# Loads, stores and pacing of the pair operands in a two-layer encoder trunk, with the SwiGLU's row scale and the query loads placed elsewhere

## The chip, the cores and the metric

The kernel runs on one core of a Trainium2 chip. Its time is the device time of one execution in microseconds (us). TensorE is called PE here, VectorE DVE, ScalarE ACT, GpSimd POOL and SyncE SP, as in the profile.

## The reference

Two request groups, one of 1024 tokens ("p", the prompt, token blocks 1 and 2 of 512 tokens) and one of 512 ("s", block 0), go through the same two layers with the same weights, in float32. Each layer is a mixer with a residual, then a SwiGLU with a residual:

```python
for i in range(DEPTH):                      # DEPTH = 2, D_MODEL = 1024, D_FF = 2816
    if i % 2 == 0:
        x = x + fourier_mixer(x, norm_mix[i], fourier_w[j])
    else:                                   # 8 query heads, 2 key heads of 128
        x = x + attention_mixer(x, norm_mix[i], attn_w_qkv[j], attn_q_norm[j],
                                attn_k_norm[j], attn_w_o[j], cos, sin)
    x = x + swiglu_ffn(x, norm_ffn[i], ffn_w_gate[i], ffn_w_up[i], ffn_w_down[i])

def swiglu_ffn(x, g, w_gate, w_up, w_down):
    h = rms_norm(x, g)
    return (jax.nn.silu(h @ w_gate) * (h @ w_up)) @ w_down
```

`rms_norm` divides each token's row by its root mean square and multiplies by a gain. The two groups don't depend on each other.

## The kernel before

**Numbers.** Activations lie with features on partitions and tokens on the free axis: a block of 512 tokens is 8 chunks of 128 x 512. Each operand of a product is split into a rounded high part and the rest (`split`, L238: ACT casts, L242, and DVE or POOL subtracts, L243). A product is three matmuls, high by high, high by low, low by high (`mm3`, L249 to L251). Weights come from DRAM by `weights_by` (L278): loads issued on SP (L283), a cast on ACT (L287), a subtraction on POOL (L288).

**Two ways of the SwiGLU.** Block 0 goes through `ffn` (L759): 22 blocks (`fc`) of 128 hidden features, each with a gate product, an up product and the element-wise part: gate by the row scale `first["r"]` on DVE (L851), up by the row scale on DVE (L852), silu on ACT (L853), silu by up on DVE (L854), and a split into `mid`. The down products of two blocks at a time wait in a list, `pend`, and are slipped between the gate and up matmuls of the next block; their results are added up on DVE (L780). Blocks with odd `fc` close a pair. Blocks 1 and 2 go through `ffn_pair` (L924), which multiplies the two blocks, and two halves of every weight, as 2 x 2 matrices of blocks with seven products in place of eight. The seven operands of the activation side (`OPERANDS`: B11, B21, T2, T1, B22, T3, N4) are sums and differences of normed chunks of the two token blocks.

**Making the pair operands.** `moving` (L871) makes them in four rounds `j`. A round loads four residual chunks (two token blocks, two halves of the features) from DRAM into one buffer `x4` (L883, on SP), multiplies them by gain and row scale on DVE (L889), and forms the operands in three thirds: first B11, B21 and B22, then T1 and T3, then T2 and N4 (subtractions on DVE, L912 to L919). `put` splits each operand; B21, T1, T3 and N4 have their subtraction on POOL (`helped`), the others on DVE. Each split operand is stored to DRAM at once (L905, on SP). B11 and B21 also stay in the `ring` in SBUF. Every third ends with `yield 5.0`. `x4` and the buffer of T2 and N4 have the same tag, `wX`, with four buffers (`BUFS`, L151).

**Weaving.** Stages are Python generators. `weave` (L1397) runs two of them, a main and an aux one. Each `yield` states a cost; the one whose stated costs are the smaller share of its whole cost goes next. So the yields set where in the program text a stage's instructions stand among the other's. In layer 0 main is `ffn` of block 0 (whole cost 352) and aux the prompt's Fourier mixer, its projection and `moving` (250). In layer 1 main is block 0's attention and `ffn` (223 + 0.85 x 352 = 522.2) and aux the prompt's attention, output projection and `moving` (630). Behind `moving`, `paired` (L1515) emits the pair's first weights; when the weave is over, the rest of `ffn_pair` is emitted.

**Order and buffers.** The order of the text is a priority, not the order of the queues: when the program is built, each engine is given, among the instructions that are ready, the one that stands first in the text. On the chip each engine works through its queue in that order, and waits where an input has not come. Buffers of one tag are handed out in the order of the text.

**Down weights of the pair.** For each pair of blocks `f0`, `load_rows_down` (L997) loads two rows of the down weight at step T1, `prepare_down` (L1031) starts their sums and splits at step B22 (first DVE product at L1017, first POOL one at L1019), and the generator behind it is continued at T3 and later.

**Attention.** `attend` (L1307) takes, for each of the 8 heads, a query (loads on SP, L1333, split by ACT and POOL), then for each 128 queries the scores, the softmax, transposed probabilities and the values. The query of a head is loaded and split at the head's start.

Of the kernel before, what the change touches and what calls it, by code (L numbers as in the profile page):

```python
# [20 lines left out]
TB = 512  # L21
# [104 lines left out]
def trunk_kernel(ctx: ExitStack, tc: tile.TileContext, t: dict):  # L126
# [632 lines left out]
    def ffn(layer, b, h, out=None):  # L759
        h = h()  # L760
        here = b in resident
        acc = resident.pop(b) if here else staying[b]
        kept[b] = acc
        yield 0.0

        def halves(ms, wds, f0, dc):

            box = []

            def half(i):  # L770
                w = wds[dc // 4].rearrange("p h (f c) n -> p h f c n", f=2)
                mm3(box[0], w[:, 0, i, dc % 4], w[:, 1, i, dc % 4], ms[i][:, 0], ms[i][:, 1], i == 0, i == 1)

            def begin():
                box.append(bank())
                half(0)

            def end():
                half(1)
                dve.tensor_tensor(acc[dc], box[0], acc[dc], op=ALU.add)  # L780
                if f0 + 2 == NF:
                    new_residual(b, dc, acc[dc], None if out is None else out[:, dc, :])

            return begin, end

        def one(n=1):
            for _ in range(n):
                if pend:
                    pend.pop(0)()

        ready = {v: first[i] for i, v in enumerate((("gate", 0), ("up", 0), ("gate", 1)))} if here else {}

        def want(v, fc):
            if fc < NF and (v, fc) not in ready:
                ready[v, fc] = weights(down_src(layer, fc, "AB".index(v)) if v in "AB" else t[v][layer, fc])

        def open_items(ms, f0):

            wds = [ready.pop(("A", f0))]
            pairs = [halves(ms, wds, f0, dc) for dc in range(NC)]  # L800
            turns = [pairs[0][0], pairs[1][0], pairs[0][1], pairs[1][1]]
            for v in pairs[2:]:
                turns.extend(v)
            pend.extend(turns)
            return wds

        wds = None
        want("gate", 0)
        want("up", 0)
        for fc in range(NF):  # L810
            f0, odd_ = fc - fc % 2, fc % 2
            wg, wu = ready.pop(("gate", fc)), ready.pop(("up", fc))
            if not odd_ and wds is not None:
                want("B", f0 - 2)
                wds.append(ready.pop(("B", f0 - 2)))
            ga, up = bankg(), bankg()
            for dc in range(NC):
                if odd_ and dc == 4:
                    want("A", f0)
                part(wg, h, ga, dc)  # L820
                if here and fc == 0:
                    part(wu, h, up, dc)
                if not odd_ and dc >= 5:
                    one()
                if dc % 2:
                    yield 1.36 if odd_ or dc < 5 else 2.0 if dc == 5 else 2.7
            if odd_:
                want("gate", fc + 1)
                wds = open_items(ms, f0)
            for dc in range(NC):  # L830
                if not odd_ and dc == 3:
                    want("gate", fc + 1)
                if fc == NF - 1 and dc == 4:
                    want("B", f0)
                if dc == (2 if odd_ else 4):
                    want("up", fc + 1)
                if fc == 0 and not here and dc == 1:
                    settled(b)
                if not (here and fc == 0):
                    part(wu, h, up, dc)  # L840
                if not odd_:
                    one(2 if dc in (2, 4, 6) else 1)
                elif dc >= 6:
                    one()
                if dc % 2:
                    yield (3.4 if dc > 1 else 2.7) if not odd_ else 2.7 if dc == 7 else 1.36
            s = tmp()
            if fc == 0 and not here:
                first["r"] = tl("ss", [TB], F32, "ssF")
                act.copy(first["r"], in_rows(rstd[b]))  # L850
            dve.tensor_tensor(ga, ga, first["r"], op=ALU.mult)  # L851
            dve.tensor_tensor(up, up, first["r"], op=ALU.mult)  # L852
            act.activation(s, ga, AF.Silu)  # L853
            dve.tensor_tensor(up, up, s, op=ALU.mult)  # L854
            m = tl("mid", [2, TB], F32R, "mid")
            split(m[:, 0], m[:, 1], up)
            if odd_:
                ms.append(m)
            else:
                ms = [m]  # L860
        want("B", NF - 2)
        wds.append(ready.pop(("B", NF - 2)))
# [8 lines left out]
    def moving(blocks, gain, out, ring, helped):  # L871

        staging = open_pool("mv")
        yield 2.0
        r = [in_rows(rstd[b]) for b in blocks]
        yield 1.0
        for j in range(4):
            x4 = tl("x", [2, 2, TB], F32, "wX")
            v = {}
            for k in range(2):  # L880
                for d in range(2):
                    x = x4[:, d, k]
                    sp.dma_start(x, xres[blocks[k]][:, 4 * d + j, :])  # L883
                    v[d, k] = x
            a2 = bank2()
            for (d, k), x in list(v.items()):
                if d == k:
                    v[d, k] = a2[:, d]
                dve.scalar_tensor_tensor(v[d, k], x, gain[:, 4 * d + j : 4 * d + j + 1], r[k], op0=ALU.mult, op1=ALU.mult)  # L889
            room = []  # L890

            def put(name, src):
                if name in OPERANDS[:2]:
                    x = ring[:, 4 * OPERANDS.index(name) + j]
                elif name == "T1":
                    x = tl("l", [2, TB], F32R, "rawX")
                elif name in ("B22", "T3"):
                    x = tl("l", [2, TB], F32R, "mv", staging)
                else:
                    if not room:  # L900
                        two = tl("l", [2, 2, TB], F32R, "wX")
                        room.extend([two[:, 0], two[:, 1]])
                    x = room.pop(0)
                split(x[:, 0], x[:, 1], src, eng=pool if name in helped else None)
                sp.dma_start(out[name][:, j], x.bitcast(F32))  # L905

            put("B11", v[0, 0])
            put("B21", v[1, 0])
            put("B22", v[1, 1])
            yield 5.0  # L910
            t1 = x4[:, 0, 0]
            dve.tensor_tensor(t1, v[0, 1], v[0, 0], op=ALU.subtract)  # L912
            put("T1", t1)
            dve.tensor_tensor(v[0, 1], v[1, 1], v[0, 1], op=ALU.subtract)
            put("T3", v[0, 1])
            yield 5.0
            dve.tensor_tensor(v[1, 1], v[1, 1], t1, op=ALU.subtract)
            put("T2", v[1, 1])
            dve.tensor_tensor(v[1, 0], v[1, 0], v[1, 1], op=ALU.subtract)  # L919
            put("N4", v[1, 0])  # L920
            yield 5.0
        close_pool("mv")

    def ffn_pair(layer, blocks, ring, places, outs):  # L924
# [106 lines left out]
        def prepare_down(f0):  # L1031

            preps.append(operands_down(f0))
            next(preps[-1])
# [140 lines left out]
        for f0 in range(0, NF, 2):  # L1175
# [20 lines left out]
                plus(U[i], ps, U[i])  # L1196
            for i, ps in (yield from step("T1", lambda: load_rows_down(f0), 0)):
                plus(V[i], ps, U[i])
            for i, ps in (yield from step("B22", lambda: prepare_down(f0), 0)):
                plus(ps, ps, V[i])  # L1200
                if i == 0:
                    s = gated(1, W, ps)
                else:
                    finish(1, ps, s)
            for i, ps in (yield from step("T3", lambda: next(preps[-1]), 0)):
                plus(U[i], ps, U[i])
                plus(ps, ps, V[i])
                if i == 0:
                    s = gated(2, V[0], ps)
                else:  # L1210
                    finish(2, ps, s)
            for i, ps in (yield from step("N4", None if f0 else lambda: load_acc(blocks[0], 0), 0)):
                plus(ps, ps, U[i])
                if i == 0:
                    s = gated(3, U[0], ps)
# [91 lines left out]
    def attend(blocks, straight, slot):  # L1307
# [6 lines left out]
        for g in range(NKV):  # L1314
# [12 lines left out]
                sp.dma_start(vr[:, n * 4 : n * 4 + 4], dv[b][g][:, :, :])  # L1327
            split(vt[:, 0], vt[:, 1], vr, eng=pool)
            yield 1.0
            for h in range(g * GROUP, (g + 1) * GROUP):  # L1330
                qr = raw_tile(T)
                for n, b in enumerate(blocks):
                    sp.dma_start(qr[:, n * TB : (n + 1) * TB], dqk[b][h][:, :])  # L1333
                qt = w_tile(2, T)
                split(qt[:, 0], qt[:, 1], qr, eng=pool)
                pts = {}

                def scores(qc):
# [45 lines left out]
                for qc in range(nk + LAG):  # L1384
                    if qc < nk:
                        ps.append(scores(qc))
                        yield 0.7 * nb
                    n = qc - LAG
                    if n >= 0:
# [294 lines left out]
```

## Time and profile before

| | |
|---|---|
| time, median of 3 runs | 2942.33 us (2935.05 to 2945.19) |
| profiled execution | 2943.94 us, span 2942.2 us |
| mean granted TensorE clock | 0.989 |
| ACT busy (share) | 1307.7 us (44%) |
| DMA | 490.53 MB, mean 167 GB/s |

The span runs from the first to the last instruction of the profiled execution. A busy time is the time in which the engine has an instruction at work; matmuls overlap, so a busy PE can still run slower than it could, and the granted clock and the count of matmuls in a stretch say more. `moving` shows itself by the lines L883, L889 and L905: its products run from 366.2 to 442 us for layer 0 and from 2180.8 to 2246 us for layer 1.

### The profile page before, as it was taken

How to read it: one execution, taken by the hardware profiler on the slowest of the kernel's cores; microseconds unless marked ns; L12 is line 12 of the kernel's file. 1: busy time of each engine (PE TensorE's matmuls, PEld its weight loads, DVE VectorE, ACT ScalarE, POOL GpSimd, SP SyncE). 2: the span in 40 equal slices, each digit the busy share in tenths (PEclk: the TensorE clock that was granted, in tenths of full speed). 3: DMA queues.
4: the chain of work that ended last, by engine and by line, in shares of the span. 5: the costliest groups of instructions: out<-in, count | busy, mean ns of one | idle time of the engine just before them, and what ended most of it. 6: DMA issues, size and time to landing. Idle time of an engine off the chain costs nothing.

```text
span 2942.2 us, 37189 instructions
## 1 busy us (share of the span) xinstructions
PE 2851.2 (97%) x13656; PEld 2350.9 (80%) x13656; DVE 1737.2 (59%) x3067; ACT 1307.7 (44%) x2134; POOL 1516.2 (52%) x932
## 2 busy tenths in 40 slices
PE   7999999999999999999999999999998999999999
PEld 6778877788888887787777888888886788888887
DVE  6674554466666666836546565563245466666666
ACT  5543233333333333546757777763233333333332
POOL 4334355676776676432332122224535667766774
PEclk8999999999999999999999999999999999999999
DMA  6435475766556653632322112115447865556553
GB/s 219 147 121 161 133 270 188 274 219 218 199 185 207 229 187 111 232 97 86 94 97 90 35 61 78 54 54 179 161 159 279 303 236 202 186 206 226 197 172 116
DMA packets 178870, 490.53 MB, mean 167 GB/s; under 512 B 19488, under 2 KB 29728, under 8 KB 177280
## 3 DMA queue, kind: packets, MB, share of 16 engines
q1 hardware_dynamic: 177760, 483.36, 48.5%
q0 software_dynamic: 640, 3.74, 0.4%
q8 instruction: 108, 1.77, 0.3%
q10 hardware_dynamic: 288, 1.05, 0.1%
q14 instruction: 74, 0.61, 0.1%
HBM read 422.01 MB, written 66.06 MB: 166 GB/s over the span
## 4 chain that ended last, share of the span: by engine, by line
PE 42%; issue 3%; DVE 3%; POOL 2%; ACT 2%; DMA 2%; SPq 0%; POOLq 0%; DVEq 0%; ACTq 0%
PE a L249 6%; PE a L251 6%; PE a L250 6%; PE c L249 5%; PE c L250 4%; PE c L251 4%; PE g L251 3%; PE g L249 3%; PE g L250 3%; PE c L1366 2%; POOL w L288 1%; DVE col L1349 1%; DMA x<-xres 1%; DVE col L1348 1%; DVE acc L1056 1%
## 5 line engine op out<-in xcount | busy, mean ns | idle before, releaser
L288 POOL TENSOR_TENSOR w<-raw,w 128x1024 fp32r<-128x1024 f32 x200 | 479.2, 2403 | 852.0 <-ACT w L287 828.9
L243 POOL TENSOR_TENSOR w<-raw,w 128x512 fp32r<-128x512 f32 (+1 forms) x464 | 607.1, 1328 | 437.8 <-ACT w L242 430.3
L242 ACT CAST w<-raw 128x512 fp32r<-128x512 f32 (+1 forms) x464 | 279.5, 632 | 533.3 <-PE a L251 174.8
L287 ACT CAST w<-raw 128x1024 fp32r<-128x1024 f32 x200 | 208.3, 1048 | 280.6 <-PE g L251 97.0
L249 PE MATMUL g<-h,w 128*128 128x512 f32 x704 | 281.1, 399 | 11.6 <-ACT w L287 6.9
L251 PE MATMUL g<-h,w 128*128 128x512 f32 x704 | 278.3, 395 | 1.2 <-POOL w L288 1.2
L249 PE MATMUL a<-ring,w 128*128 128x512 f32 x708 | 277.5, 392 | 0.0
L250 PE MATMUL g<-h,w 128*128 128x512 f32 x704 | 277.5, 394 | 0.0
L251 PE MATMUL a<-ring,w 128*128 128x512 f32 x708 | 276.0, 390 | 0.0
L250 PE MATMUL a<-ring,w 128*128 128x512 f32 x708 | 275.8, 390 | 0.0
L1056 DVE TENSOR_TENSOR acc<-g,acc 128x512 f32<-128x512 f32 x294 | 201.7, 686 | 105.2 <-PE g L251 104.9
L1056 DVE TENSOR_TENSOR acc<-c,acc 128x512 f32<-128x512 f32 x294 | 201.6, 686 | 93.2 <-PE c L251 91.5
L249 PE MATMUL c<-mid,w 128*128 128x512 f32 x604 | 237.4, 394 | 13.5 <-ACT mid L242 9.5
L250 PE MATMUL c<-mid,w 128*128 128x512 f32 x604 | 236.7, 392 | 1.3 <-DVE mid L243 1.1
L251 PE MATMUL c<-mid,w 128*128 128x512 f32 x604 | 236.4, 392 | 0.0
L249 PE MATMUL c<-h,w 128*128 128x512 f32 x480 | 191.5, 400 | 4.4 <-ACT h L245 3.5
L250 PE MATMUL c<-h,w 128*128 128x512 f32 x480 | 189.7, 396 | 0.4
L251 PE MATMUL c<-h,w 128*128 128x512 f32 x480 | 189.3, 395 | 0.0
L780 DVE TENSOR_TENSOR acc<-c,acc 128x512 f32<-128x512 f32 x176 | 120.8, 688 | 112.6 <-PE c L251 111.9
L249 PEld LDWEIGHTS g<-h,w 128*128 128x128 f32 x704 | 133.7, 190 | 39.3 <-ACT w L287 7.3
L249 PEld LDWEIGHTS a<-ring,w 128*128 128x128 f32 x708 | 133.1, 188 | 32.2 <-DVE mid L243 4.3
L251 PEld LDWEIGHTS g<-h,w 128*128 128x128 f32 x704 | 133.3, 189 | 29.1 <-POOL w L288 2.0
(393 smaller groups left out, 6712.5 us busy)
## 6 DMA issues: line engine op xcount, KB each, us to landing
ring<-mov_B SPq DMA_DIRECT2D x248, 512.0 KB, 5.5
ring<-mov_T SPq DMA_DIRECT2D x88, 512.0 KB, 5.3
raw<-in_gate_dram SPq DMA_DIRECT2D x44, 512.0 KB, 3.5
raw<-in_up_dram SPq DMA_DIRECT2D x44, 512.0 KB, 3.5
raw<-in_down_dram SPq DMA_DIRECT2D x88, 256.0 KB, 3.0
raw<-in_gate_dram SPq DMA_DIRECT2D x88, 256.0 KB, 5.3
raw<-in_up_dram SPq DMA_DIRECT2D x88, 256.0 KB, 5.6
raw<-in_down_dram SPq DMA_DIRECT2D x44, 512.0 KB, 4.2
```

The costliest lines, as they stand in the source:

```text
L242: keep(act.copy(hi, src))
L243: keep(eng.tensor_tensor(lo, src, hi.bitcast(F32), op=ALU.subtract))
L249: pe.matmul(out, lh, rh, start=first, stop=False, **kw)
L250: pe.matmul(out, lh, rl, start=False, stop=False, **kw)
L251: pe.matmul(out, ll, rh, start=False, stop=last, **kw)
L287: pinned(act.copy(flat[:, 0], raw)) if early else act.copy(flat[:, 0], raw)
L288: pool.tensor_tensor(flat[:, 1], raw, flat[:, 0].bitcast(F32), op=ALU.subtract)
L780: dve.tensor_tensor(acc[dc], box[0], acc[dc], op=ALU.add)
L1056: dve.tensor_tensor(acc, chain[d], acc, op=ALU.add)
L1348: dve.tensor_reduce(st[:, 2 * kb : 2 * kb + 1], sc[:, kb], op=ALU.max, axis=AX.X)
L1349: dve.scalar_tensor_tensor(st[:, 1:2], st[:, 2 * nb - 2 : 2 * nb - 1], st[:, 0:1], nrqc[:, gq, h : h + 1], op0=ALU.max, op1=ALU.mult)
L1366: pe.transpose(tr[:, i * P : (i + 1) * P], p[:, kc * P : (kc + 1) * P], ident)
```

## The change

- `moving`: the chunks of round 0 are loaded before the loop, those of round `j + 1` after B22 of round `j`, by a helper `load`. The stores are put on a list and issued by `flush` after the next `yield`, a third later. Each third ends with `yield 9.0` in place of `5.0`.
- `ffn`: up is no longer multiplied by the row scale; silu's result is, on POOL.
- `ffn_pair`: for the first pair of blocks (`f0` 0) `prepare_down` comes at step T3 and its continuation at N4, each one step later.
- `attend`: the query of a head's successor in the same group is loaded and split halfway through the head's scores.

```diff
@@ -849,8 +849,8 @@
                 first["r"] = tl("ss", [TB], F32, "ssF")
                 act.copy(first["r"], in_rows(rstd[b]))
             dve.tensor_tensor(ga, ga, first["r"], op=ALU.mult)
-            dve.tensor_tensor(up, up, first["r"], op=ALU.mult)
             act.activation(s, ga, AF.Silu)
+            pool.tensor_tensor(s, s, first["r"], op=ALU.mult)
             dve.tensor_tensor(up, up, s, op=ALU.mult)
             m = tl("mid", [2, TB], F32R, "mid")
             split(m[:, 0], m[:, 1], up)
@@ -873,15 +873,28 @@
         staging = open_pool("mv")
         yield 2.0
         r = [in_rows(rstd[b]) for b in blocks]
+        stores = []
+
+        def flush():
+            for dst, x in stores:
+                sp.dma_start(dst, x.bitcast(F32))
+            stores.clear()
+
+        def load(j):
+
+            x4, v = tl("x", [2, 2, TB], F32, "wX"), {}
+            for k in range(2):
+                for d in range(2):
+                    v[d, k] = x4[:, d, k]
+                    sp.dma_start(v[d, k], xres[blocks[k]][:, 4 * d + j, :])
+            loaded.append((x4, v))
+
+        loaded = []
+        load(0)
         yield 1.0
         for j in range(4):
-            x4 = tl("x", [2, 2, TB], F32, "wX")
-            v = {}
-            for k in range(2):
-                for d in range(2):
-                    x = x4[:, d, k]
-                    sp.dma_start(x, xres[blocks[k]][:, 4 * d + j, :])
-                    v[d, k] = x
+            flush()
+            x4, v = loaded.pop()
             a2 = bank2()
             for (d, k), x in list(v.items()):
                 if d == k:
@@ -902,23 +915,28 @@
                         room.extend([two[:, 0], two[:, 1]])
                     x = room.pop(0)
                 split(x[:, 0], x[:, 1], src, eng=pool if name in helped else None)
-                sp.dma_start(out[name][:, j], x.bitcast(F32))
+                stores.append((out[name][:, j], x))
 
             put("B11", v[0, 0])
             put("B21", v[1, 0])
             put("B22", v[1, 1])
-            yield 5.0
+            if j < 3:
+                load(j + 1)
+            yield 9.0
+            flush()
             t1 = x4[:, 0, 0]
             dve.tensor_tensor(t1, v[0, 1], v[0, 0], op=ALU.subtract)
             put("T1", t1)
             dve.tensor_tensor(v[0, 1], v[1, 1], v[0, 1], op=ALU.subtract)
             put("T3", v[0, 1])
-            yield 5.0
+            yield 9.0
+            flush()
             dve.tensor_tensor(v[1, 1], v[1, 1], t1, op=ALU.subtract)
             put("T2", v[1, 1])
             dve.tensor_tensor(v[1, 0], v[1, 0], v[1, 1], op=ALU.subtract)
             put("N4", v[1, 0])
-            yield 5.0
+            yield 9.0
+        flush()
         close_pool("mv")
 
     def ffn_pair(layer, blocks, ring, places, outs):
@@ -1196,20 +1214,20 @@
                 plus(U[i], ps, U[i])
             for i, ps in (yield from step("T1", lambda: load_rows_down(f0), 0)):
                 plus(V[i], ps, U[i])
-            for i, ps in (yield from step("B22", lambda: prepare_down(f0), 0)):
+            for i, ps in (yield from step("B22", (lambda: prepare_down(f0)) if f0 else None, 0)):
                 plus(ps, ps, V[i])
                 if i == 0:
                     s = gated(1, W, ps)
                 else:
                     finish(1, ps, s)
-            for i, ps in (yield from step("T3", lambda: next(preps[-1]), 0)):
+            for i, ps in (yield from step("T3", (lambda: next(preps[-1])) if f0 else lambda: prepare_down(0), 0)):
                 plus(U[i], ps, U[i])
                 plus(ps, ps, V[i])
                 if i == 0:
                     s = gated(2, V[0], ps)
                 else:
                     finish(2, ps, s)
-            for i, ps in (yield from step("N4", None if f0 else lambda: load_acc(blocks[0], 0), 0)):
+            for i, ps in (yield from step("N4", None if f0 else lambda: (load_acc(blocks[0], 0), next(preps[-1])), 0)):
                 plus(ps, ps, U[i])
                 if i == 0:
                     s = gated(3, U[0], ps)
@@ -1327,12 +1345,17 @@
                 sp.dma_start(vr[:, n * 4 : n * 4 + 4], dv[b][g][:, :, :])
             split(vt[:, 0], vt[:, 1], vr, eng=pool)
             yield 1.0
-            for h in range(g * GROUP, (g + 1) * GROUP):
+            def query(h):
                 qr = raw_tile(T)
                 for n, b in enumerate(blocks):
                     sp.dma_start(qr[:, n * TB : (n + 1) * TB], dqk[b][h][:, :])
                 qt = w_tile(2, T)
                 split(qt[:, 0], qt[:, 1], qr, eng=pool)
+                return qt
+
+            hq = {g * GROUP: query(g * GROUP)}
+            for h in range(g * GROUP, (g + 1) * GROUP):
+                qt = hq.pop(h)
                 pts = {}
 
                 def scores(qc):
@@ -1384,6 +1407,8 @@
                 for qc in range(nk + LAG):
                     if qc < nk:
                         ps.append(scores(qc))
+                        if qc == nk // 2 and h + 1 < (g + 1) * GROUP:
+                            hq[h + 1] = query(h + 1)
                         yield 0.7 * nb
                     n = qc - LAG
                     if n >= 0:
```

## The prediction

> **What bounds the kernel now.** I read the page first, then the busy time by stretches of 25 us, then who waited for whom, then the timelines of VectorE, SyncE, ScalarE and GpSimd around the holes.
>
> ```profile
> PE 2851.2 (97%) x13656; PEld 2350.9 (80%) x13656; DVE 1737.2 (59%) x3067; ACT 1307.7 (44%) x2134; POOL 1516.2 (52%) x932
> ```
>
> TensorE (PE) is busy for 97% of the span. The change removes no matmul, so all it can win is the time in which PE stands still or runs at a lower clock. The span is 2942.2 us, so PE idles 91 us in all. What matters is which part of that the change touches: the two stretches in which `moving` makes the pair operands, the two changeovers to `ffn_pair` behind them, the SwiGLU blocks, and attention. From the busy time by stretch (columns: stretch, its length, then busy us and count for PE, PEld, DVE, ACT, POOL, the granted clock, the DMA share, GB/s):
>
> ```profile
> 400.00:425.00 25.00, 21.73 (x88) 17.15 (x87) 14.71 (x23) 8.80 (x14) 15.77 (x10) 0.93 0.77 282
> 425.00:450.00 25.00, 22.56 (x100) 18.38 (x99) 13.74 (x22) 10.64 (x15) 14.78 (x9) 1.00 0.84 291
> ...
> 475.00:500.00 25.00, 25.00 (x112) 20.68 (x111) 9.18 (x14) 5.46 (x7) 11.32 (x5) 1.00 0.26 83
> ...
> 525.00:550.00 25.00, 22.85 (x101) 18.35 (x100) 9.98 (x15) 7.67 (x11) 18.02 (x9) 1.00 0.62 210
> ```
> ```profile
> 2225.00:2250.00 25.00, 17.40 (x71) 12.92 (x70) 15.00 (x25) 11.56 (x19) 14.31 (x10) 0.92 0.79 284
> 2250.00:2275.00 25.00, 24.38 (x95) 19.69 (x96) 10.42 (x16) 6.89 (x10) 12.07 (x8) 0.87 0.73 253
> 2275.00:2300.00 25.00, 20.81 (x82) 16.66 (x80) 6.25 (x10) 3.99 (x7) 17.26 (x9) 0.86 0.73 251
> ```
>
> The row 475 to 500 is a full one: the SwiGLU alone, 112 matmuls in 25 us, 0.223 us each. Missing matmuls price a hole together with the slower clock that follows it. In the two `moving` stretches 24, 12, 41 and 17 are missing, 94 x 0.223 = 21.0 us. In the two changeovers (525 to 550 and 2275 to 2300) 11 and 30 are missing, 9.1 us. In 2225 to 2275 the idle time is 8.2 us and the missing matmuls are worth 12.9 us: a long hole costs about 1.6 times its length.
>
> What ends these holes? VectorE (DVE), which works through its queue in order, shows it:
>
> ```profile
> 413.34 0.76 DVE L889 SCALAR_TENSOR_TENSOR a<-x,gains,c 128x512 f32<-128x512 f32 x1 [5.04 <-DMA x<-xres]
> ```
> ```profile
> 439.05 0.76 DVE L889 SCALAR_TENSOR_TENSOR a<-x,gains,c 128x512 f32<-128x512 f32 x1 [6.64 <-DMA x<-xres]
> ```
> ```profile
> 2242.48 0.75 DVE L889 SCALAR_TENSOR_TENSOR a<-x,gains,c 128x512 f32<-128x512 f32 x1 [7.30 <-DMA x<-xres]
> ```
>
> Three times DVE stands 5 to 7 us at the first product of a round because the residual chunk has not landed. Behind it in the queue lie the SwiGLU's own evictions and products, and behind those, through ScalarE's casts, PE. The chunk is late because its load is issued last in the round, and SyncE (SP), also in order, stands for stores ahead of it:
>
> ```profile
> 2230.51 4.40 SPq L905 DMA_DIRECT2D mov_T<-l  x3
> 2237.86 0.32 SPq L905 DMA_DIRECT2D mov_N<-l  x1
> 2238.22 2.23 SPq L883 DMA_DIRECT2D x<-xres  x4
> 2240.49 0.43 SPq L283 DMA_DIRECT2D raw<-in_gate_dram  x1
> ```
> ```profile
> 2248.16 0.80 PE L249 MATMUL g<-h,w 128*128 128x512 f32 x1 [6.89 <-ACT w L287]
> ```
>
> The four x loads follow the last store within 0.4 us, and the SwiGLU's next gate weight follows them. PE stood 6.89 us until 2248.16, waiting for that weight's cast. So the worst hole has two causes, the x load in front of DVE and the queue in front of the weight.
>
> **The change part by part.** The sum stands against the profiled execution's 2943.94 us (span 2942.2 and 1.7 around it), 1.6 above the median of the three runs.
>
> *x half a round ahead.* The same 16 loads per layer pass, in the program text, from behind the round's last stores to behind its third operand. They pass SP's two later groups of stores, and their buffer is taken before the one of T2 and N4 instead of after it. That instructions are really issued ahead of their place in the text when buffer and inputs allow is seen here:
>
> ```profile
> 308.82 1.27 SPq L883 DMA_DIRECT2D x<-xres  x3
> ```
> ```profile
> L889 DVE SCALAR_TENSOR_TENSOR a<-x,gains,c x8: 746/752/756, 366.2 to 441.6; 128x512 f32<-128x512 f32 x8
> ```
>
> The load of round 0 is issued at 308.8, its first product starts at 366.2. So the loads of round 1 can go as early, and those of rounds 2 and 3 a round ahead; a round takes 25.7 us here (413.34 to 439.05), far more than the load, whose DVE waits are 5 to 7 us. All three DVE waits should go. Worth: at most the 21.0 us. At least 0, if the weight in SP's queue is late anyway. In the worst hole, the gate weight at 2240.49 comes forward by the 2.6 us since 2237.86 that the x loads take, to a hole of about 4 instead of 7 us and no further. I leave 6 of the 21 standing and take -15.
>
> *Stores a third behind.* The same 28 stores per layer, but behind the next third's loads. They still wait on SP for GpSimd's (POOL) splits:
>
> ```profile
> SPq L905 <- POOL l L243: 38.7, 22, 5.5
> ```
> ```profile
> SPq L905 <- POOL ring L243: 23.2, 8, 5.2
> ```
>
> 62 us of waiting in some 160 us of `moving`: what is queued behind is the SwiGLU's weights. If all of it goes, the 6 us that I left go too; if none goes, they stay. I take 0 here. Their source buffers are held a third longer, which has the next third's buffer of T1 or T3 wait at worst; the spread of the rounds covers that.
>
> *More SwiGLU beside (9 for 5 in each of twelve yields).* No instruction is added. Moving's end comes later against the SwiGLU: 48 units more, in the second layer 48 x 522.2/630 = 39.8 us of SwiGLU. Whether that leaves cover is a rival, below. In the forecast the rounds follow their inputs, not the yields, as the early load showed: 0, up to +14 by that rival.
>
> *Row scale on silu's result.* Per block one DVE multiplication goes (up by the row), and one on POOL comes, between silu and the last product:
>
> ```profile
> L852 DVE TENSOR_TENSOR g<-g,ss 128x512 f32<-128x512 f32 x44 | 30.6, 696 | 30.7 <-PE g L251 30.3
> ```
> ```profile
> L243 POOL TENSOR_TENSOR l<-x,l 128x512 fp32r<-128x512 f32 x24 | 30.6, 1297 | 3.9 <-ACT l L242 3.8
> ```
>
> DVE loses 44 x 0.70 = 31 us, POOL gains 44 x 1.30 = 57 us. Neither is the bound. What counts is the tail after the up product, where PE waits for `mid` when it has nothing else. There 0.8 us goes (start of up by row to start of up by silu, below), if POOL delivers in time. The tight case is the odd block:
>
> ```profile
> 501.71 0.59 ACT L853 ACTIVATE t<-g 128x512 f32<-128x512 f32 x1
> ```
> ```profile
> 501.89 2.39 POOL L288 TENSOR_TENSOR w<-raw,w 128x1024 fp32r<-128x1024 f32 x1 [2.35 <-ACT w L287]
> ```
> ```profile
> 505.83 0.70 DVE L852 TENSOR_TENSOR g<-g,ss 128x512 f32<-128x512 f32 x1 [5.42 <-PE g L251]
> 506.63 0.70 DVE L854 TENSOR_TENSOR g<-g,t 128x512 f32<-128x512 f32 x1
> 507.98 0.69 DVE L243 TENSOR_TENSOR mid<-g,mid 128x512 fp32r<-128x512 f32 x1 [0.65 <-ACT mid L242]
> 511.27 0.69 DVE L780 TENSOR_TENSOR acc<-c,acc 128x512 f32<-128x512 f32 x1 [2.59 <-PE c L251]
> ```
>
> Silu ends at 502.3, POOL is free of the weight split at 504.28, the scale would end at 505.58, and the up product is done at 505.83. It fits, with 0.25 us. The `mid` of this block is complete at 508.67. PE reads it from about 510.6 (the sum at 511.27 less three matmuls), 1.9 us later. So POOL may be about 3 us late (0.25 + 1.9 + 0.8) before PE feels it: one more weight split of 2.39, not two. I take -1, for the two changeovers; bounds -2 and the third rival.
>
> The Trainium skill speaks against this part: GPSIMD Engine Reference, section Engine selection, gives elementwise work on a tile to VectorE, GpSimd being about twice as slow with two inputs. The rows agree (1.297 to 0.696 us). By that rule taken as path time the 44 scales would cost 44 x 0.60 = 26 us instead of my -1. The third rival is that rule as a mechanism of this kernel.
>
> *The first `prepare_down` a step later.* At both changeovers DVE ran a product of it ahead of the SwiGLU's last block:
>
> ```profile
> 540.52 0.69 DVE L1017 TENSOR_TENSOR s<-raw,raw 128x512 f32<-128x512 f32 x1 [7.47 <-DMA raw<-in_up_dram]
> ```
> ```profile
> 2289.45 0.69 DVE L1017 TENSOR_TENSOR s<-raw,raw 128x512 f32<-128x512 f32 x1 [9.51 <-DMA raw<-in_gate_dram]
> 2290.06 0.69 DVE L852 TENSOR_TENSOR g<-g,ss 128x512 f32<-128x512 f32 x1
> ```
>
> DVE stood for its weights, and the last up by row behind it. Those are the changeovers' 9.1 us. The product was issued well ahead of its place in the text, so a place one step later may change nothing. Bounds 0 and -9.1; I take -2.5.
>
> *Queries ahead.* In attention PE waits for a split operand here:
>
> ```profile
> PE g L251 <- POOL w L243: 2.1, 4, 0.6
> ...
> PE a L251 <- POOL w L243: 1.3, 1, 1.3
> ```
>
> 3.4 us, part of it for keys, which are not moved. For one-block attention the second query takes the fourth of four buffers, and the second transposed tile then waits for the first one's reader; PE issues in order there and reads it first. Bounds -3.4 and +2; I take -1.5.
>
> Sum: -15 - 1 - 2.5 - 1.5 = -20, so 2924 for the profiled execution, and 2923 beside the median.
>
> **The rivals.** *The wait moves to the stores.* The 62 us of SP's waiting stay, the SwiGLU's weights stay late, and the holes shrink by a third only: 21 x 1/3 = -7, with nothing from the changeovers: 2936. For it: order on SP follows readiness, so putting stores later in the text need not put them later in the queue. Against: in all three holes DVE waits for x.
>
> *The pair starts without cover.* If the rounds keep to the yields, `moving` ends 39.8 us of SwiGLU later in layer two. Before, this much lay between its last store and the last SwiGLU block:
>
> ```profile
> 2256.64 0.44 SPq L905 DMA_DIRECT2D mov_N<-l  x1
> ...
> 2261.32 0.33 SPq L1101 DMA_DIRECT2D raw<-in_gate_dram  x1
> ```
> ```profile
> raw<-in_gate_dram SPq DMA_DIRECT2D x88, 256.0 KB, 5.3
> ```
>
> 2290.06 - 2256.64 = 33.4 us, so nothing is left. From the last store to the pair's first matmul: 4.7 to its load, 5.3 to land, two splits of 1.3 on POOL, 12.6 us, times 1.6 for the clock 20, less the 6.7 us that this changeover loses already: +13. With -15 and -1: 2941, about no change. Layer one has room: 48 x 352/250 = 67.6 of the 99 us from its last product at 441.6 to 540.52.
>
> *POOL late: slower.* If on the odd blocks POOL is two weight splits behind (4.8 us, where 3 are free), `mid` is 1.8 us late 22 times, 39 us; with the -18 of the rest +21: 2965. It decides from 3 us on. Against: POOL is 52% busy over the span. For: in `moving` it has four more splits a round.
>
> **How the numbers follow.** A measurement of this kernel can tell 0.3%, 9 us, from no change. Forecast 0.56, stores 0.20, pair start 0.13, POOL 0.11. Faster by over 0.3% (under 2933.5): nine tenths of the forecast, a third of each of the next two: 0.62. Slower (above 2951): three quarters of the POOL case and a little of the pair start: 0.10. The same: 0.28. The range reaches down to all bounds together (-21 - 2 - 9 - 3 = -35, 2907) and up over the pair start to 2945.
>
> **What would show it.** Right: no DVE wait for x beyond round 0; over 105 matmuls in each 25 us of both `moving` stretches; the clock at 1.00 there. Wrong: SP standing for L905 with weights behind it; a hole of over 8 us before the pair's first matmul; PE waiting for `mid` in the middle of the SwiGLU with POOL as the last link.

## The result and the profile after

The changed kernel takes 2919.31 us in the median of 5 runs (2916.32 to 2928.02), the kernel before 2941.85 us on the same chip (5 runs, 2935.05 to 2945.19). The ratio is 0.9934 with the interval 0.9919 to 0.9948: faster by 0.7%, some 19 us (the two medians alone differ by 22.5). The forecast was 2923, a gain of 20.

The profiled execution of after took 2916.32 us (span 2914.5, granted clock 0.996), 27.6 us less than that of before. Some of these 27.6 us are the two executions and not the kernels: the last section shows how much their first 50 us differ. The first row of the page:

```profile
PE 2834.5 (97%) x13656; PEld 2341.5 (80%) x13656; DVE 1714.5 (59%) x3023; ACT 1304.7 (45%) x2134; POOL 1573.4 (54%) x976
```

The matmuls are the same 13656. DVE has 44 instructions fewer and POOL 44 more, which is the row scale. Where PE gained, the stretches tell. First the two of before that the prediction didn't need, then those of after (columns as in the prediction):

```profile
450.00:475.00 25.00, 25.00 (x112) 20.70 (x111) 9.41 (x14) 7.75 (x12) 14.42 (x9) 1.00 0.89 310
...
2200.00:2225.00 25.00, 24.14 (x105) 19.36 (x104) 16.32 (x26) 9.33 (x14) 13.31 (x8) 1.00 0.88 314
```
```profile
400.00:425.00 25.00, 24.05 (x106) 19.44 (x105) 16.11 (x25) 9.65 (x14) 16.97 (x11) 1.00 0.77 286
425.00:450.00 25.00, 24.63 (x108) 19.83 (x107) 6.92 (x10) 5.78 (x7) 14.33 (x8) 1.00 0.87 309
450.00:475.00 25.00, 24.54 (x107) 19.74 (x106) 6.86 (x10) 7.20 (x9) 13.93 (x7) 1.00 0.52 194
525.00:550.00 25.00, 23.89 (x106) 19.36 (x105) 10.64 (x16) 8.73 (x16) 20.50 (x13) 1.00 0.87 298
...
2200.00:2225.00 25.00, 24.08 (x106) 19.96 (x107) 18.09 (x29) 12.74 (x19) 21.45 (x14) 1.00 0.83 291
2225.00:2250.00 25.00, 25.00 (x112) 20.68 (x111) 8.93 (x13) 6.70 (x8) 12.90 (x7) 1.00 0.81 281
2250.00:2275.00 25.00, 20.92 (x86) 16.77 (x85) 5.16 (x7) 3.75 (x8) 17.28 (x11) 0.93 0.84 303
2275.00:2300.00 25.00, 25.00 (x112) 20.71 (x111) 9.41 (x14) 8.42 (x17) 16.36 (x12) 1.00 0.96 342
```

Count what is missing from 112 in these eight stretches. Before: 24, 12, 0, 11, 7, 41, 17, 30, together 142. After: 6, 4, 5, 6, 6, 0, 26, 0, together 53. The 89 matmuls times 0.223 us are 19.8 us, about the measured gain. So the time came from where the prediction looked for it. One hole is left, the 26 in 2250 to 2275: that is the second layer's changeover to `ffn_pair`.

What stood in front of the weights on SP? In after, the same part of SP's timeline as the prediction showed (the first products of the second layer now start at 2167.3 in place of 2180.8; L880 are the stores, L889 the x loads):

```profile
2192.11 0.33 SPq L283 DMA_DIRECT2D raw<-in_gate_dram  x1
2194.62 1.58 SPq L880 DMA_DIRECT2D mov_T<-l  x2
2199.51 0.33 SPq L283 DMA_DIRECT2D raw<-in_up_dram  x1
...
2200.83 3.72 SPq L889 DMA_DIRECT2D x<-xres  x4
2205.88 0.81 SPq L283 DMA_DIRECT2D raw<-in_down_dram  x2
2210.74 0.33 SPq L283 DMA_DIRECT2D raw<-in_gate_dram  x1
...
2224.96 0.59 SPq L283 DMA_DIRECT2D raw<-in_gate_dram  x1
```

and in before, ahead of the late gate weight at 2240.49:

```profile
2208.96 0.33 SPq L283 DMA_DIRECT2D raw<-in_gate_dram  x1
2212.56 2.07 SPq L905 DMA_DIRECT2D mov_T<-l  x3
...
2215.51 3.50 SPq L883 DMA_DIRECT2D x<-xres  x4
```

After loads a gate weight of the SwiGLU every 14 to 19 us (2192.11, 2210.74, 2224.96). Before let 31.5 us pass between two of them (2208.96 to 2240.49), and in that time issued the stores and x loads of more than a whole round. One part of the change, or several, brought the weights forward. The prediction held it to be the x loads. The experiments say otherwise.

### The profile page after: what moved, and what is told of

It reads as the page before. It is cut to its first block, busy times and chain, and to the rows that moved or that the text cites. A ratio compares the mean times of both kernels' runs of the same rounds, so it can differ in the third digit from the quotient of the medians.

```text
span 2914.5 us, 37209 instructions
## 1 busy us (share of the span) xinstructions
PE 2834.5 (97%) x13656; PEld 2341.5 (80%) x13656; DVE 1714.5 (59%) x3023; ACT 1304.7 (45%) x2134; POOL 1573.4 (54%) x976
## 4 chain that ended last, share of the span: by engine, by line
PE 44%; DVE 3%; issue 2%; ACT 1%; DMA 1%; POOL 1%; SPq 0%; POOLq 0%; DVEq 0%; ACTq 0%
PE a L249 6%; PE a L251 6%; PE a L250 6%; PE c L249 5%; PE c L250 5%; PE c L251 5%; PE g L251 3%; PE g L249 3%; PE g L250 3%; PE c L1389 2%; DVE col L1372 1%; DVE col L1371 1%; DVE acc L1074 1%; POOL w L288 0%; ACT p L1375 0%
## 5 line engine op out<-in xcount | busy, mean ns | idle before, releaser
L249 PEld LDWEIGHTS a<-ring,w 128*128 128x128 f32 x708 | 133.0, 188 | 32.1 <-DVE mid L243 4.3
L249 PEld LDWEIGHTS g<-h,w 128*128 128x128 f32 x704 | 132.5, 188 | 30.1 <-DVE ss L339 2.2
L251 PEld LDWEIGHTS a<-ring,w 128*128 128x128 f32 x708 | 133.1, 188 | 27.9
```

What stands on the lines that cost most here:

```text
L249: pe.matmul(out, lh, rh, start=first, stop=False, **kw)
L251: pe.matmul(out, ll, rh, start=False, stop=last, **kw)
```

## The experiments

Two theories. The **load theory** is the prediction's: DVE stands for the residual chunk, the SwiGLU's evictions stand behind DVE, so loading x earlier brings the gain. The **place theory**: the SwiGLU's weights are late on SP, because `moving`'s instructions stand too early in the text; what brings the gain is the larger number in the yields, which puts them further back among the SwiGLU's, whether or not x is early. The recorded expectations name two more. The **queue theory**: SP's 62 us of standing for operands that it is to store hold the weights back. The **spread theory**: the larger number stretches `moving` over more time.

All ratios are to the kernel before on the same chip, with their 95% intervals. The last two columns count the matmuls missing from 112 per 25 us in one profiled execution of each, in 400 to 450 (`moving` of the first layer) and in 2200 to 2300 (`moving` and changeover of the second layer).

| kernel | yields | x | stores | the rest of the change | ratio (95%) | first layer | second layer |
|---|---|---|---|---|---|---|---|
| before | 5 | late | at once | no | 1 | 36 | 95 |
| e1_x_ahead | 5 | ahead | at once | no | 0.9975 (0.9966 to 0.9984) | 5 | 73 |
| e4_yields5 | 5 | ahead | behind | yes | 0.9979 (0.9969 to 0.9989) | 16 | 79 |
| e10_yields9 | 9 | late | at once | no | 0.9931 (0.9919 to 0.9944) | 32 | 17 |
| e5_x_late | 9 | late | behind | yes | 0.9935 (0.9921 to 0.9950) | 31 | 25 |
| e11_x_yields9 | 9 | ahead | at once | no | 0.9931 (0.9918 to 0.9943) | 7 | 25 |
| e7_stores_now | 9 | ahead | at once | yes | 0.9922 (0.9907 to 0.9937) | 12 | 10 |
| e2_moving | 9 | ahead | behind | no | 0.9921 (0.9906 to 0.9937) | 8 | 24 |
| after | 9 | ahead | behind | yes | 0.9934 (0.9919 to 0.9948) | 10 | 32 |
| e12_x_yields13 | 13 | ahead | at once | no | 0.9922 (0.9908 to 0.9935) | 8 | 34 |

Every row with 5 has 0.9975 or more, every row with 9 or 13 has 0.9935 or less, and the intervals of the two groups don't touch. With 5, x ahead brings 7 us. With 9 or 13, neither x nor the stores nor the rest of the change make a difference that can be told.

Two more numbers from the second layer's part of the same traces go with the yields. The longest time between two of the SwiGLU's gate loads, counted from the first product of `moving`, is 28.8 to 35.0 us in before, e1 and e4, and 17.2 to 21.5 us in the seven kernels with 9 or 13. PE's waits for a weight's cast or split between 2165 and 2300 are 8.1, 7.7 and 9.1 us in before, e1 and e4, and none in the seven. Was it a buffer that the late gate weight lacked? In the three long gaps SP stood 0.9, 2.9 and 0 us for the buffer of a SwiGLU weight (L283), and 13 to 19 us in front of stores.

**x ahead alone.** On the kernel before:

```diff
+        load(0)
         for j in range(4):
-            x4 = ...            # four loads of round j
+            x4, v = loaded.pop()
...
             put("B22", v[1, 1])
+            if j < 3:
+                load(j + 1)
             yield 5.0
```

> The kernel before with the x loads half a round ahead and nothing else of the change (stores at once, yields of 5). If the DVE waits for x are the cause (load theory): 15 us less than before, ratio 0.995, DVE idle for x under 10 us instead of 27.5. If SP's standing for the stores is the cause (queue theory): 3 us less at most, SP still waits some 60 us for the stores' splits.

Measured 2931.67 us against 2939.21: 0.9975, so 7 us and not 15. The load theory holds in the first layer: from 36 missing matmuls to 5. In the second layer the hole is still there; it has moved. One stretch, two of PE's waits and two of SP's gate weights, of this kernel:

```profile
2200.00:2225.00 25.00, 17.70 (x62) 12.97 (x63) 17.79 (x29) 10.49 (x18) 12.54 (x9) 0.86 1.02 388
```
```profile
2217.61 0.50 PE L249 MATMUL c<-mid,w 128*128 128x512 f32 x1 [3.01 <-ACT w L287]
2220.05 0.80 PE L251 MATMUL c<-mid,w 128*128 128x512 f32 x1 [1.59 <-POOL w L288]
```
```profile
2177.83 0.33 SPq L283 DMA_DIRECT2D raw<-in_gate_dram  x1
2212.81 1.05 SPq L283 DMA_DIRECT2D raw<-in_gate_dram  x1
```

Of PE's 7.5 us of waits in this stretch 6.2 are for casts and splits of weights and 1.3 for `mid`. The gate weight came 35.0 us after the one before it, later than in the kernel before: SP issued 19 stores and 8 x loads of `moving` in between, where the 31.5 us of before had 11 and 8. DVE's waits for x are down to 9.0 us, as the load theory had it. SP's waits for the stores' splits fell too, to 20.3 us, where the queue theory had them stay at some 60.

**The three edits of `moving` together**, without row scale, `prepare_down` and queries:

```diff
+                stores.append((out[name][:, j], x))    # and flush() after the next yield
+                load(j + 1)                            # after B22
-            yield 5.0
+            yield 9.0                                  # three times
```

> The kernel before with all three changes to moving (x ahead, stores a third behind, yields of 9), without row scale, prepare_down and queries. Load theory: as much as x ahead alone, about 15 us less. Queue theory: 15 us less here and much less with x ahead alone. Both: over 105 matmuls in each 25 us of both moving stretches.

Measured 0.9921, 23 us: all of the gain is here, and none that can be told in the other edits.

**After, with the yields back at 5:**

```diff
-            yield 9.0
+            yield 5.0      # three times
```

> The changed kernel with the yields of moving back at 5. If the rounds follow their inputs and not the yields: the same as the changed kernel (ratio to before 0.9934) within 4 us, and moving's products end within 10 us of where they end with 9. If the yields of 9 spread the load (spread theory): 8 us or more above the changed kernel.

Measured 2931.39 us, 0.9979: two thirds of the gain are gone with three numbers. The prediction had given them nothing, since "the rounds follow their inputs, not the yields". That is half right. The products of the second layer and its last stores (N4's) by the one and the other, e4 first, after second:

```profile
L902 DVE SCALAR_TENSOR_TENSOR a<-x,gains,c x8: 745/750/757, 2170.1 to 2208.0; 128x512 f32<-128x512 f32 x8
```
```profile
L880 SPq DMA_DIRECT2D mov_N<-l x4: 320/391/792, 2184.1 to 2224.1; - x4
```
```profile
L902 DVE SCALAR_TENSOR_TENSOR a<-x,gains,c x8: 745/748/756, 2167.3 to 2211.3; 128x512 f32<-128x512 f32 x8
```
```profile
L880 SPq DMA_DIRECT2D mov_N<-l x4: 320/422/968, 2185.0 to 2243.1; - x4
```

The last product comes at 2208.0 and 2211.3: nearly twice the stated cost moves it by 3 us. The last store comes at 2224.1 and 2243.1, 19 us apart, half of the 39.8 us of the stated costs. So the end of `moving` does follow the yields in part, and the spread theory, which asked for 8 us or more here and got 13 by the ratios, isn't excluded by this run; the next but one tells it from the place theory. The yields also moved the order of what shares the queue with `moving`. The gate weights of e4:

```profile
2178.34 0.33 SPq L283 DMA_DIRECT2D raw<-in_gate_dram  x1
2207.14 1.12 SPq L283 DMA_DIRECT2D raw<-in_gate_dram  x1
```

28.8 us lie between them, and PE waited for weights again (3.0 and 2.4 us for casts, 2.0 and 1.7 for splits).

**After, with x back at the start of its round:**

```diff
-        load(0)
         for j in range(4):
             flush()
+            load(j)
...
-            if j < 3:
-                load(j + 1)
```

> The changed kernel with the x loads of each round back at the round's start in the text. Load theory: 12 to 15 us above the changed kernel (ratio to before 0.998), the DVE waits for x back above 20 us. Queue theory: within 4 us of the changed kernel.

Measured 0.9935 against after's 0.9934. The load theory falls as the cause of the gain. DVE does stand for x, 12.4 us in the second layer alone, and the rounds take 69 us from the first product to the last in place of after's 44, with no cost in the whole that can be told:

```profile
L902 DVE SCALAR_TENSOR_TENSOR a<-x,gains,c x8: 750/756/757, 2182.8 to 2251.9; 128x512 f32<-128x512 f32 x8
...
  DMA x<-xres: 12.4, 8
```

**The yields alone**, three numbers in the kernel before:

```diff
-            yield 5.0
+            yield 9.0      # three times
```

> The kernel before with only the yields of moving raised from 5 to 9. Load theory, already shaken: within 4 us of before, ratio above 0.9985. Place theory (the yields put the SwiGLU's weight loads ahead of moving's instructions wherever both are ready, and that is most of the gain): ratio 0.994, though DVE's waits for x stay above 20 us; the stretches of moving end as late as before or later.

Measured 2915.99 us against 2938.2: 0.9931, 20 us, all of the change's gain. DVE's wait for x in both layers, the gate weights and the stretches of this kernel:

```profile
  DMA x<-xres: 20.1, 9
```
```profile
2196.61 0.33 SPq L283 DMA_DIRECT2D raw<-in_gate_dram  x1
2215.61 0.33 SPq L283 DMA_DIRECT2D raw<-in_gate_dram  x1
2232.95 0.43 SPq L283 DMA_DIRECT2D raw<-in_gate_dram  x1
```
```profile
425.00:450.00 25.00, 21.94 (x85) 17.58 (x84) 13.74 (x21) 8.48 (x12) 12.25 (x7) 0.86 0.74 244
...
2225.00:2250.00 25.00, 23.27 (x103) 18.96 (x102) 14.38 (x23) 9.99 (x15) 16.76 (x10) 1.00 0.84 302
2250.00:2275.00 25.00, 25.00 (x111) 20.39 (x110) 9.49 (x14) 6.98 (x12) 18.29 (x10) 1.00 0.98 354
```

The gate weights come every 17 to 19 us, as in after. In the second layer 78 of the 95 missing matmuls are back (17.4 us), with DVE still waiting 9.6 us for x there (14.3 in before), though at most 3.43 us at a time (7.30 in before). In the first layer the hole for x stays (27 missing in 425 to 450). The place theory holds. The spread theory has little to stand on: from the first product to the last store of the second layer 75.8 us passed in before and 80.5 here.

**x ahead with the yields at 9**, the e1 and e10 edits together:

```diff
+                load(j + 1)     # after B22
-            yield 5.0
+            yield 9.0           # three times
```

> The kernel before with x ahead and yields of 9 and nothing else: stores at once, no row scale, prepare_down or queries. Place theory: 0.992, as with all of moving's changes (0.9921), so the deferred stores, row scale, prepare_down and queries add nothing together. If the stores matter: 0.9945 or above.

Measured 0.9931, the same as without x ahead. That is no proof that x ahead does nothing. The stretches of this kernel:

```profile
425.00:450.00 25.00, 25.00 (x112) 20.72 (x111) 10.71 (x16) 7.36 (x10) 12.76 (x8) 1.00 0.91 316
...
2250.00:2275.00 25.00, 21.25 (x87) 17.09 (x86) 6.15 (x9) 6.22 (x12) 15.21 (x10) 0.93 0.86 315
```
```profile
2260.16 0.69 DVE L1035 TENSOR_TENSOR s<-raw,raw 128x512 f32<-128x512 f32 x1 [8.62 <-DMA raw<-in_gate_dram]
```

It closes the first layer's hole (27 matmuls to none), and at the second layer's changeover a hole of 25 opens that e10 doesn't have. `moving` is over earlier, DVE comes to the pair's first sum (L1035) earlier, and stands 8.6 us for its weight, with the SwiGLU's last evictions behind it. On this reading the gain is given back. That the same hole of 24 to 26 is in e2, after and e12, all with x ahead, speaks for this; e7 has only 8 there, and e5, with x late, has 15, so its size is not settled by x alone.

**Yields of 13**, the same with 13:

```diff
-            yield 5.0
+            yield 13.0      # three times, x ahead as above
```

> The same with yields of 13, so that moving's text ends 79.6 us of SwiGLU later in the second layer, with some 35 us there. If the rounds follow their inputs: within 4 us of the yields of 9, moving's products end at the same time. If the pair's start loses its cover (rival of the prediction): a hole of 12 us or more before the pair's first matmuls in the second layer, 13 us above the yields of 9.

Measured 0.9922, not to be told from 9. From the last store of `moving` to the last SwiGLU block's up by row scale (L852) 15.7 us are left here and 21.5 in e11; before had 33.4, of which the rival left nothing at 9. So the cover shrinks, by far less than the stated costs, and no larger hole came up (24 missing, 25 in e11). The rival of a pair without cover is refuted at 9 and at 13.

**After, with stores at once:**

```diff
-                stores.append((out[name][:, j], x))
+                sp.dma_start(out[name][:, j], x.bitcast(F32))
```

> The changed kernel with the stores issued at once again (x ahead and yields of 9 stay). Load theory: within 4 us of the changed kernel (ratio to before 0.994), though SP's waits for the stores' splits return to some 50 us. Queue theory: 10 us or more above the changed kernel.

Measured 0.9922 (after 0.9934; the intervals overlap): the stores a third behind are worth nothing that can be told. SP's wait for the splits on POOL that it stores fell from the 38.7 and 23.2 us of before to this, in after:

```profile
SPq L880 <- POOL l L243: 7.1, 7, 2.1
...
SPq L880 <- POOL ring L243: 3.4, 2, 1.8
```

With the stores at once, here, they are 10.7 and 5.7 us, not the 50 expected. So most of the fall came with the early x (20.3 in e1), and the later stores took some 6 us off. In e10, which has the whole gain, these waits are 28.4 and 20.1 us. With both, the queue theory falls: in e1 two thirds of the waiting went and a third of the gain came, in e10 most of the waiting stayed and all of the gain came.

**Row scale alone**, on the kernel before:

```diff
-            dve.tensor_tensor(up, up, first["r"], op=ALU.mult)
             act.activation(s, ga, AF.Silu)
+            pool.tensor_tensor(s, s, first["r"], op=ALU.mult)
```

> The kernel before with only the row scale moved to silu's result on POOL. By my sum 1 us less, not to be told from no change. By the rule that elementwise work belongs on VectorE, taken as path time, 26 us more.

Measured 0.9995 (0.9985 to 1.0005): between 4 us less and 1 more, no difference that can be told.

**After, with the first `prepare_down` back at B22:**

```diff
-            ... step("B22", (lambda: prepare_down(f0)) if f0 else None, 0)
+            ... step("B22", lambda: prepare_down(f0), 0)      # T3 and N4 likewise
```

> The changed kernel with the first prepare_down back at step B22. My sum has 2.5 us for this step, so 2.5 us above the changed kernel; if its place in the text does nothing, as the hole of 4.1 us that is still there in the second layer suggests, 0.

Measured 0.9939 (0.9926 to 0.9953) against after's 0.9934: the step later is worth nothing that can be told (2.5 us could hide in these intervals). After's own trace gives a reason. At the changeover DVE still ran a sum of it ahead of the SwiGLU's last `mid`, as in before:

```profile
2259.10 0.70 DVE L854 TENSOR_TENSOR g<-g,t 128x512 f32<-128x512 f32 x1 [5.48 <-PE g L251]
...
2264.09 1.08 DVE L1035 TENSOR_TENSOR s<-raw,raw 128x512 f32<-128x512 f32 x1 [4.29 <-DMA raw<-in_gate_dram]
2265.10 0.68 DVE L243 TENSOR_TENSOR mid<-g,mid 128x512 fp32r<-128x512 f32 x1
```
```profile
2265.83 0.79 PE L250 MATMUL c<-mid,w 128*128 128x512 f32 x1 [4.08 <-DVE mid L243]
```

PE lost 4.1 us there, waiting for `mid`, and with the clock (0.93) 26 matmuls.

**After, with that sum held to its place in the text:**

```diff
-            dve.tensor_tensor(s1, a21, a22, op=ALU.add)
+            ins = dve.tensor_tensor(s1, a21, a22, op=ALU.add)
+            if not f0:
+                pinned(ins)
```

> The changed kernel with the first DVE sum of prepare_down held, for the first pair of blocks, to its place in the text on DVE, so that it can't go ahead of the SwiGLU's last block. If it is what makes PE wait 4.1 us at the second changeover: that hole goes, 5 to 6 us less than the changed kernel (26 missing matmuls there), ratio to before 0.9915. If something else makes the last mid late: no change.

Measured 0.9955 (0.9941 to 0.9969): no gain, if anything a little less than after. The hole at 2250 to 2275 went, with 112 matmuls there. Another came 50 us later, of this kernel:

```profile
2300.00:2325.00 25.00, 22.69 (x93) 18.03 (x92) 16.43 (x24) 9.99 (x18) 16.61 (x12) 0.93 0.73 288
```
```profile
PE g L249 <- ACT mid L242: 2.3, 1, 2.3
```

The hole was moved, not removed. The held sum runs there as well, at 2309.30; whether it is what made `mid` late at the new place is not shown.

**Queries alone**, the `attend` edit of the change on the kernel before:

```diff
+                        if qc == nk // 2 and h + 1 < (g + 1) * GROUP:
+                            hq[h + 1] = query(h + 1)
```

> The kernel before with only the queries taken half a head ahead. By my sum 1.5 us less, bounds -3.4 and +2: not to be told from no change. PE's waits for split operands in attention down from 4 us to under 2.

Measured 0.9990 (0.9982 to 0.9999): 3 us, between 0.3 and 5.3, inside the 0.3% that one can't tell from none. PE's waits for POOL's split operands there were 3.4 us before and are 2.6 here (1.4 and 1.2), not under 2 as expected, so the trace accounts for under 1 us of it.

## Why the prediction was right, and which step of it failed

The time was right, and so were the mechanism's place (PE's holes in the two `moving` stretches and the changeovers), the price of a hole in missing matmuls, and the sum of -20. The cause was put down to the wrong edit. That the sum came out all the same is luck: a term of 15 that is worth less, and one of 0 that is worth 20 alone, made up for each other.

*x half a round ahead, -15.* This is the step that failed. "In all three holes DVE waits for x" was read from the trace and was so; that PE's holes go when those waits go was concluded from it. For the first layer it is true: e1 and e11 close that hole (25 to 31 matmuls, 6 to 7 us). In the second, the larger part, two things came late together in before. The weight that PE waited 6.89 us for landed about 2247.0 (issued at 2240.49, 6.5 us to landing), and its cast stood on ACT right behind one that had waited for the round's x:

```profile
2246.58 0.59 ACT L242 CAST ring<-a 128x512 fp32r<-128x512 f32 x1 [1.65 <-DVE a L889]
2247.06 1.05 ACT L287 CAST w<-raw 128x1024 fp32r<-128x1024 f32 x1
```

So an early x alone could not close the hole. In e1 x is early, the weight is still late, and 73 of the 95 matmuls are missing. In e10 and e5 the weights come in time, DVE still waits for x, but no more than 4.0 us at once, and 17 and 25 are missing. The prediction saw the "two causes", and had as its lower bound that "the weight in SP's queue is late anyway". It gave the queue in front of the weight only the 2.6 us of x loads, and left 6 of 21 us to it. In the second layer the late weight by itself kept most of the hole open; whether x late by 7 us would have, with the weight in time, no run shows. Alone x ahead brought 7 us, on top of the new yields nothing that can be told (0.9931 both ways); the hole at the changeover, as large as the first layer's, would explain that.

*More SwiGLU beside, 0.* The term that carried the gain: 20 us by itself in e10. The premise, that the rounds follow their inputs, was confirmed by e4 for the products (3 us), and half so for the last store (19 of 39.8 us). The conclusion didn't follow. A yield that decides only in part when a stage ends still decides the place in the text, and so which of two ready instructions a queue in order takes first. At 5, `moving`'s stores and loads came first on SP and the SwiGLU's weights after them. How much of this is SP's order and how much DVE's and POOL's, where the same priority holds, no run here separates.

*Stores a third behind, 0.* Right (e7), and for the reason given in the rival's disfavour: the sum of 62 us of SP's waiting was not what held the holes open. It fell to 10 in after, to 16 with the stores at once (e7), and remained 48 in e10, which is as fast. The rival "the wait moves to the stores" is refuted by e10.

*Row scale, -1.* Right within what e3 can tell. In after the 44 scales on POOL and what waited for them:

```profile
L853 POOL TENSOR_TENSOR t<-t,ss x44: 1280/1289/1326, 107.8 to 2256.2; 128x512 f32<-128x512 f32 x44
...
  DVE g L854: 26.2, 5
```

1.289 us each, where DVE took 0.696. The Trainium skill (GPSIMD Engine Reference, section Engine selection) gives GpSimd as about twice as slow with two inputs, and the trace about agrees. As path time it would have been 26 us more; e3's interval ends at 1. DVE did stand 26.2 us for POOL, at five places, but the sum of PE's waits for `mid` didn't grow (13.5 us in before, 14.1 with the row scale alone in e3, 8.3 in after). The rival of a late POOL is refuted.

*`prepare_down`, -2.5.* Nothing that can be told (e9), though 2.5 us would not have shown either. The prediction's doubt, that the product is issued ahead of its place anyway, is what after's trace shows.

*Queries, -1.5.* Not distinguishable from right.

*The signs.* The clock is 1.00 in the `moving` stretches and their rows have 106 to 112 matmuls, as said. DVE's waits for x did not quite go: three are left, 7.4 us together, and they cost little. Their sum was no sign: e5 and e10 have 20 us and more of these waits, and the same time as after. Of the signs of being wrong, the hole before the pair's first matmul was there with 4.1 us, where over 8 were named.

## What to carry to other kernels

Read the wait of the engine that bounds the kernel first, and ask whether a second one ends at the same time: here PE's own wait named a weight's cast, the louder wait was DVE's for x, both ended together in the larger of the two places, and taking one away left the other. Where two stages share a queue that works in order, check how far apart the main stage's loads are issued (31.5 us in before, 17 to 22 at most in the fast kernels), since the aux stage's instructions can stand in front of them without showing as a wait of the main stage's loads. And test the parts of a bundled change alone: three numbers had the whole gain, and the kernel with only those three is as fast as any other here.

## What the runs showed of the hardware that was not expected

The start of an execution varies more than most edits here bring. The stretch 25 to 50 us, which no part of the change touches, in before, after and e12_x_yields13:

```profile
25.00:50.00 25.00, 16.62 (x43) 11.48 (x44) 19.63 (x37) 16.08 (x29) 13.94 (x7) 0.55 0.61 192
```
```profile
25.00:50.00 25.00, 17.71 (x69) 12.62 (x70) 20.59 (x34) 18.31 (x34) 13.97 (x9) 0.73 0.71 210
```
```profile
25.00:50.00 25.00, 16.20 (x41) 11.07 (x42) 19.47 (x37) 16.08 (x29) 13.51 (x7) 0.56 0.57 179
```

The 26 matmuls between before and after are some 6 us of the 27.6 us between their profiled executions, which goes far to explain why these differ by more than the medians' 22.5. A kernel with nothing changed but the queries had 48 there, one with the yields alone 71. PE is busy for about the same time in the two rows shown first; what differs is the granted clock, 0.55 and 0.73. Each kernel has one such profile, but the executions of one kernel differ as well: before took 2934.15 to 2944.68 us in fifteen runs on one chip, with mean granted clocks of 0.992 and 0.989 in these two. Why it is granted less in some executions, no run here shows.
